# Hybrid state-space and attention block on one core: the down projection's last 256 tokens with tokens on partitions, their norm from a square root, and a new order of the first loads

## The chip, the cores and the metric

The kernel runs on 1 core of a Trainium2 chip. The metric is the device time of one execution in microseconds (us). Five engines work side by side, each through its own instructions in order: TensorE (PE, matrix products), VectorE (DVE), ScalarE (ACT), GpSimd (POOL) and SyncE (SP), which here does nothing but start DMA transfers between the chip's main memory and the on-chip memory. ACT and POOL can start transfers too. Engines wait for one another by semaphores. On-chip data lie on 128 partitions.

## The reference

One layer: a norm, a projection into two groups of heads (a diagonal state-space model and chunked attention with a window of 9 chunks of 64 frames), an output projection with a residual, a norm, a SwiGLU feed-forward layer with a residual, and a final norm over the 1024 features of each of 2048 tokens. Only the start and the end of it matter here:

```python
D_MODEL = 1024; SEQ = 2048; EPS = 1e-6

def rmsnorm(x, g):
    y = x * lax.rsqrt(jnp.mean(x * x, axis=-1, keepdims=True) + EPS)
    return y * g

# start:  h = rmsnorm(x, norm_mix_g) @ w_in
# end:    x = x + (silu(h2 @ w_gate) * (h2 @ w_up)) @ w_down
#         out = rmsnorm(x, norm_final_g)
```

All data are float32. Output: (1, 2048, 1024).

## The kernel before, in words

Activations lie with features on partitions and tokens along the free dimension: a tile is 128 features by up to 512 tokens. Each float32 operand of a large product is split into a rounded high part and a low part, and a product of two is three matrix instructions (high by high, high by low, low by high), which `mm3` issues at line 76. The transposes and the instructions at line 79 come from the same helper. Engines run in the order in which a scheduler has put the program; `tc.high_priority()` moves a group ahead there.

**Start.** `block_kernel` issues, all on SP: the three gains `g_mix`, `g_ffn`, `g_final` (L1666) and the relative bias `nbt` (L1670), which DVE negates (L1671) and SP stores back as `nbs` (L1672). `u_phase` then loads, for the first block of tokens, eight pairs of a weight tile `w` (L437) and an input tile `xt` (L441). ACT casts the weight's high part `wuh` (L438) and scales the input by `g_mix` into `raw` (L443); PE starts with the first pair.

**Middle.** The down phase and the gate and up phase before it fetch their operands with SP (`lo<-hc`, L1363, is 20 loads at the boundary after the output projection; `xt<-in_xt`, L1133, follows; DVE adds into `xt` at L1141, and PE's first `X<-hi,c` of the next phase waits for that).

**End.** `down_phase` walks the hidden features in groups and adds each group's product into the accumulators `acc` (8 tiles of 128 features by 1024 tokens, for each of two halves of the tokens). For the second half the last group of hidden features is kept back in the on-chip tiles `hs` and `ds`, and `TAIL` gives the order of what is left: three chunks of tokens, (first token, count) = (0, 512), (512, 256), (768, 256). I call them chunk 1, 2 and 3. For each chunk `down` makes tiles 0 to 3, then 4 and 5, then 6 and 7 of its 8 feature tiles, 12 matrix instructions a tile; DVE adds each into `acc` (L1575), ACT squares it (L1589, L1592), DVE adds the squares into `sa` and `sb` (L1593). Behind tiles 0 to 3 of a chunk come the `sums` of the chunk before it: PE sums the squares over the partitions by products with a column of ones, which puts tokens on partitions; `newton` turns that into the reciprocal root by 14 small DVE operations (L102 to L110, a bit trick and three Newton steps); behind tiles 4 and 5 PE spreads the root over all partitions by a transpose (L79), ACT copies it to `rs` (L141), and `products` multiplies each `acc` tile by gain and root on DVE (L1605) and stores it from SP (L1606). After chunk 3 there is no later chunk: its sums, root, products and stores follow one another.

Of the kernel before, what the change touches and what calls it, by code (L numbers as in the profile page):

```python
# [25 lines left out]
H, HD = 8, 64  # L26
# [4 lines left out]
HALF = 1024  # L31
# [20 lines left out]
ORDER = "sptf"  # L52
PINA = True
X1B = 6
TAIL = (0, 512), (512, 256), (768, 256)
MAGIC = 12582912.0
F2 = NF // 2
SB_, CB_, GB_ = 5, 5, 10
# [39 lines left out]
def newton(k, pool, ps, n, w):  # L98

    V = k.nc.vector  # L100
    v, f, y, o = (k.t(pool, t, [P, w], bufs=2) for t in ("nv", "nf", "ny", "no"))
    V.tensor_scalar(v[:], ps, 1.0 / n, EPS, op0=ALU.mult, op1=ALU.add)  # L102
    V.tensor_copy(f[:], v[:].bitcast(I32))
    V.tensor_scalar(f[:], f[:], -0.5, 1597463007.0, op0=ALU.mult, op1=ALU.add)
    V.tensor_copy(y[:].bitcast(I32), f[:])
    V.tensor_scalar(v[:], v[:], -0.5, None, op0=ALU.mult)
    for a, b in ((y, o), (o, y), (y, o)):
        V.tensor_tensor(f[:], a[:], a[:], op=ALU.mult)
        V.tensor_tensor(f[:], f[:], v[:], op=ALU.mult)
        V.scalar_tensor_tensor(b[:], f[:], 1.5, a[:], op0=ALU.add, op1=ALU.mult)  # L110
    return o


def tok_sums(k, te, ps, c, sq):

    for i in range(4):
        te.matmul(ps[:, c + i : c + i + 1], sq[:, i * P : (i + 1) * P], k.ones[:], start=True, stop=True)
# [5 lines left out]
        te.transpose(pb[:, i * P : (i + 1) * P], o[:, c + i : c + i + 1].to_broadcast([P, P]), k.ident[:])  # L123


def rstd_steps(k, te, psum, pool, tag, sq, n, out, nt=None, **kw):

    nt = nt or out.shape[-1] // P
    ps = k.t(psum, *tag, **kw)
    sqs = sq if isinstance(sq, list) else [sq]  # L130
    for i in range(nt):
        for m, sq in enumerate(sqs):
            te.matmul(ps[:, i : i + 1], sq[:, i * P : (i + 1) * P], k.ones[:], start=m == 0, stop=m == len(sqs) - 1)
    with k.tc.high_priority():
        o = newton(k, pool, ps[:, :nt], n, nt)
    yield
    pb = k.t(psum, *tag, **kw)
    for i in range(nt):
        te.transpose(pb[:, i * P : (i + 1) * P], o[:, i : i + 1].to_broadcast([P, P]), k.ident[:])
    if out is not None:  # L140
        k.nc.scalar.copy(out, pb[:, : nt * P])  # L141
    yield pb
# [255 lines left out]
def u_phase(k, ident, S, aw):  # L398
# [3 lines left out]
    with ExitStack() as cx:  # L402
# [98 lines left out]

        pro = ssm_prologue(k, ident, S)
        next(pro)
        held = [k.t(psum, "ps", [P, SB]) for _ in range(4)]

        def first(q):
# [3 lines left out]
        xs = [k.t(aw, "w", [P, 2, 1024], bufs=WB) for _ in range(2)]  # L510
        xns = cycle([x[:, m] for x in xs for m in range(2)])
        prep(BLOCKS[0], first)
        with tc.high_priority(offset=-LATER):
            next(pro)
        sums(BLOCKS[0])
# [991 lines left out]
def down_phase(k, S):  # L1507
    tc, nc, io = k.tc, k.nc, k.io
    V, te = nc.vector, k.te
    with ExitStack() as cx:  # L1510
# [67 lines left out]
        class End:  # L1578
# [13 lines left out]
                    nc.scalar.activation(t[:, :n], self.acc[i][:, self.ts], AF.Square)  # L1592
                    nc.vector.tensor_tensor(self.sa[m][:, :n], self.sa[m][:, :n], t[:, :n], op=ALU.add)  # L1593

            def sums(self, last=False):
                self.rs = None if last else k.t(fa, "rs", [P, 512])
                self.r = rstd_steps(k, k.te, dy, fa, ("ps", [P, 512]), self.sa, D, self.rs[:, : self.n] if self.rs else None, nt=self.n // P)
                next(self.r)

            def products(self):  # L1600
                pb = next(self.r)
                rs = self.rs or pb
                for i, a in enumerate(self.acc):
                    v = a[:, self.ts]
                    nc.vector.scalar_tensor_tensor(v, v, k.go[:, i : i + 1], rs[:, : self.n], op0=ALU.mult, op1=ALU.mult)  # L1605
                    nc.sync.dma_start(io["out"][i * P : (i + 1) * P, self.out], a[:, self.ts])  # L1606

        ends = []
        for hf in range(2):
            acc = []  # L1610
            f0 = 0
            for n, g in enumerate(DGROUPS[hf]):
                group(hf, f0, g, acc, (hf, n) == (0, 0))
                f0 += g
                if n in (0, 1):
                    for e in ends:
                        (e.sums, e.products)[n]()
            if hf == 0:
                ends = [End(hf, acc, t, 512) for t in (0, 512)]
                for e in ends:  # L1620
                    for i in range(KT):
                        e.square(i)
        hs, ds = zip(*((operand(S["h"][m : m + 1]), operand(S["wt"][m : m + 1])) for m in range(4)))
        last = None
        for t0, tn in TAIL:
            e = End(1, acc, t0, tn)
            for n, i in enumerate((0, 4, 6)):
                down(hs, ds, range(i, (4, 6, 8)[n]), acc, t0, tn, e)
                if last and n < 2:
                    (last.sums, last.products)[n]()  # L1630
            last = e
        last.sums(True)
        last.products()


def block_kernel(tc, io, phases="pusamf"):
    nc = tc.nc
    k = K(tc, io)
    k.ssm_eng = nc.gpsimd
    with ExitStack() as cx:  # L1640
        dram = cx.enter_context(tc.tile_pool(name="dram", bufs=1, space=bass.MemoryType.DRAM))
        cp = cx.enter_context(tc.tile_pool(name="const", bufs=1))
        k.t(cx.enter_context(tc.tile_pool(name="edge", bufs=1, side="right")), "edge", [P, 56])

# [12 lines left out]
        k.psum = None  # L1657
        k.names = {n: a.tensor.name for n, a in S.items()}
        ident = k.t(cp, "ident", [P, P])
        make_identity(nc, ident)  # L1660
        k.ident = ident
        k.ones = k.t(cp, "ones", [P, 1])
        nc.vector.memset(k.ones[:], 1.0)
        k.gm, k.gf, k.go = (k.t(cp, n, [P, KT]) for n in ("g_mix", "g_ffn", "g_final"))
        for n, g in (("g_mix", k.gm), ("g_ffn", k.gf), ("g_final", k.go)):
            nc.sync.dma_start(g[:], io[n])  # L1666
        S["rsn"] = k.t(cp, "rsn", [P, SEQ])
        with tc.tile_pool(name="nbp", bufs=1) as p:
            nbt = k.t(p, "nbt", [H, 768])
            nc.sync.dma_start(nbt[:], io["rel_bias"])  # L1670
            nc.vector.tensor_scalar(nbt[:], nbt[:], -1.0, None, op0=ALU.mult)  # L1671
            nc.sync.dma_start(S["nb"][:], nbt[:])  # L1672
        with tc.tile_pool(name="powers", bufs=1) as p:
            S["a8"] = k.t(p, "a8", [P, 2, NPR, 16])
            S["sw"] = k.t(p, "sw", [P, 3, 2, NPR])
            S["nba"] = k.t(p, "nba", [P, 640])
            with tc.tile_pool(name="apf", bufs=2, space=bass.MemoryType.PSUM, reuse_waits="tile") as k.pfs:
                pro, att = u_phase(k, ident, S, tc.alloc_tile_pool(name="aw", reuse_waits="tile", bufs=1, side="right"))
                mix = att.send(pro)
                for _ in att:  # L1680
                    pass
        with tc.tile_pool(name="mf", reuse_waits="tile", bufs=1) as mf:
            with pp() as psum, tc.tile_pool(name="mx", reuse_waits="tile", bufs=1) as mx:
                k.psum, k.mf, k.mx = psum, mf, mx
                for _ in mix:
                    pass
            gate_up_phase(k, S)
            down_phase(k, S)
    return k


def layout(inputs):
# [7 lines left out]
    def cols(v):  # L1700
        return np.ascontiguousarray(v.reshape(-1, P).T)
# [6 lines left out]
    def cg(v):  # L1708
# [6 lines left out]
        "x": x, "xt": a["x"][0].T, "xp": x.T, "w_u": cg(a["w_in"][0][:, :DS].T).T,  # L1715
        "w_qk": blocks(a["w_in"][0][:, DS : 3 * DS], D, P), "w_v": blocks(a["w_in"][0][:, 3 * DS :], D // 2, 256), "w_glu": cg(cg(a["ssm_w_glu"][0]).T).T, "w_out": np.concatenate([cg(a["w_out"][0][:DS]), a["w_out"][0][DS:]]),
        "w_gate": blocks(a["w_gate"][0], D, P), "w_up": blocks(a["w_up"][0], D, P), "w_down": a["w_down"][0],
        "g_mix": cols(a["norm_mix_g"][0]), "g_ffn": cols(a["norm_ffn_g"][0]), "g_final": cols(a["norm_final_g"]),
        "g_ssm": cols(cg(a["norm_ssm_out_g"][0])), "g_att": cols(a["norm_att_out_g"][0]), "b_glu": cols(cg(a["ssm_b_glu"][0])),
        "lam_re": pairs(a["ssm_lam_re"][0])[:, :, 0], "lam_im": pairs(a["ssm_lam_im"][0])[:, :, 0],  # L1720
        "log_dt": pairs(np.repeat(a["ssm_log_dt"][0][:, None], NS, 1))[:, :, 0],
# [24 lines left out]
```

## Time and profile before

| what | value |
|---|---|
| time, median of 3 runs | 2256.09 us (2250.8 to 2256.18) |
| the profiled execution's own time | 2247.43 us |
| its span in the trace | 2245.7 us |
| granted TensorE clock, mean | 0.988 |
| PE busy, share of the span | 96% |
| DVE, ACT, POOL busy | 69%, 45%, 16% |
| DMA, mean over the span | 192 GB/s |

A row of a timeline gives start, duration, engine, line, operation, output tile, input tiles, shapes, how many instructions were joined in the row, and in brackets how long the engine had been idle and what released it. "SPq" is SP starting a transfer. A duration covers an instruction from start to end; instructions of one engine overlap, so the distance between starts (or a joined row's length over its count) is the price of one more.

### The profile page before, as it was taken

To read this page: it belongs to the slowest core of one execution; us is meant where nothing else is said; L and a number is where in the kernel's file an instruction comes from. 1 tells how busy PE (TensorE), PEld (TensorE's weight loads), DVE (VectorE), ACT (ScalarE), POOL (GpSimd) and SP (SyncE) were. 2 spreads that over 40 slices of the span, in tenths; PEclk is the share of its full clock that TensorE was granted. 3 is DMA by queue.
4 is the path that set the end of the run, shared out by engine and by line. 5 is a ranking of instruction groups with operands and counts; after the bars stand their busy time and mean duration, and the time that the engine had idled before them with its cause. 6 is when DMAs were issued, how large, how long until landed. Compare 5 with 4: busy or idle time off the path is not lost.

```text
span 2245.7 us, 30154 instructions
## 1 busy us (share of the span) xinstructions
PE 2155.6 (96%) x10632; PEld 1817.4 (81%) x10632; DVE 1543.3 (69%) x2706; ACT 1004.6 (45%) x1667; POOL 352.4 (16%) x827
## 2 busy tenths in 40 slices
PE   8998899999997999999999999999999999999997
PEld 6777788899986788788888887888888788888886
DVE  7756666555557766777766678767666477689776
ACT  5455555556557642443333335333333343353322
POOL 2246576656500000000000000000000100000000
PEclk9999999999998999999999999999999999999999
DMA  8878876666652435845655557646333395465652
GB/s 281 251 244 275 280 220 204 202 192 199 190 166 99 155 113 181 288 136 155 198 168 194 191 182 268 210 144 213 117 100 112 122 383 192 160 228 177 220 175 76
DMA packets 194744, 430.16 MB, mean 192 GB/s; under 512 B 19872, under 2 KB 38352, under 8 KB 187488
## 3 DMA queue, kind: packets, MB, share of 16 engines
q1 hardware_dynamic: 186944, 403.32, 54.4%
q0 software_dynamic: 7648, 24.92, 3.6%
q8 instruction: 83, 1.36, 0.2%
q14 instruction: 69, 0.57, 0.1%
HBM read 288.95 MB, written 131.10 MB: 187 GB/s over the span
## 4 chain that ended last, share of the span: by engine, by line
PE 81%; DVE 7%; DMA 4%; ACT 3%; issue 2%; SPq 0%; DVEq 0%; ACTq 0%
PE X L76 20%; PE ps L76 19%; PE Y L76 10%; PE pf L76 10%; PE big L76 7%; PE W L76 5%; PE pj L76 4%; PE pt L79 2%; PE sc L76 2%; DMA lo<-hc 1%; DMA xt<-in_xt 1%; DVE ptl L893 1%; DMA x<-xt 0%; DVE s L874 0%; DVE lo L153 0%
## 5 line engine op out<-in xcount | busy, mean ns | idle before, releaser
L76 PE MATMUL X<-hi,c 128*128 128x512 f32 x1408 | 449.8, 390 | 6.7 <-DVE c L153 3.9
L76 PE MATMUL ps<-hd,hd 128*128 128x512 f32 (+1 forms) x1968 | 428.1, 379 | 3.1 <-DVE hd L153 2.0
L76 PEld LDWEIGHTS ps<-hd,hd 128*128 128x128 f32 x1968 | 356.4, 188 | 73.3 <-DVE hd L153 2.7
L76 PEld LDWEIGHTS X<-hi,c 128*128 128x128 f32 x1408 | 264.5, 188 | 63.2 <-DVE c L153 4.7
L76 PE MATMUL X<-lo,c 128*128 128x512 f32 x704 | 274.4, 390 | 0.0
L153 ACT CAST hd<-hd 128x1536 fp32r<-128x1536 f32 (+1 forms) x106 | 147.5, 1394 | 229.9 <-DMA hd<-hq 175.5
L76 PE MATMUL Y<-hi,c 128*128 128x512 f32 x704 | 224.8, 390 | 3.1 <-DVE u L1421 2.5
L153 DVE TENSOR_TENSOR hd<-hd 128x1536 fp32r<-128x1536 f32 (+1 forms) x106 | 174.0, 1643 | 38.0 <-ACT hd L153 37.7
L153 DVE TENSOR_TENSOR c<-S,c 128x512 fp32r<-128x512 f32 x176 | 120.8, 687 | 100.1 <-ACT c L153 99.8
L1525 POOL DMA_DIRECT2D hd<-hq x7 | 5.3, 755 | 1161.5 <-PE X L76 1148.8
L1417 ACT COPY u<-X 128x512 f32<-128x512 f32 x132 | 77.3, 586 | 197.7 <-PE X L76 197.7
L153 ACT CAST c<-S 128x512 fp32r<-128x512 f32 x176 | 109.4, 621 | 120.5 <-PE Y L76 61.6
L76 PE MATMUL big<-m,woh 128*128 128x512 f32 x512 | 160.1, 394 | 0.0
L76 PEld LDWEIGHTS Y<-hi,c 128*128 128x128 f32 x704 | 132.4, 188 | 31.9 <-DVE u L1421 3.3
L1559 DVE TENSOR_TENSOR acc<-acc,ps 128x512 f32<-128x512 f32 x196 | 129.6, 680 | 37.3 <-PE ps L76 37.1
L76 PEld LDWEIGHTS X<-lo,c 128*128 128x128 f32 x704 | 132.4, 188 | 27.4
L76 PE MATMUL pf<-hi,w 128*128 128x512 f32 x416 | 149.3, 411 | 0.0
L153 ACT CAST c<-raw 128x512 fp32r<-128x512 f32 x132 | 82.2, 623 | 147.7 <-PE Y L76 70.6
L76 PE MATMUL Y<-lo,c 128*128 128x512 f32 x352 | 137.2, 390 | 0.0
L893 DVE TENSOR_TENSOR ptl<-pt,pth 128x640 fp32r<-128x640 f32 (+3 forms) x152 | 98.2, 646 | 55.2 <-ACT pth L892 53.8
L877 ACT ACTIVATE s<-s,mn 128x640 f32<-128x640 f32 (+4 forms) x128 | 98.0, 765 | 61.1 <-DVE mn L874 57.7
L892 ACT CAST pth<-pt 128x640 fp32r<-128x640 f32 (+3 forms) x152 | 83.6, 550 | 84.2 <-PE pt L79 79.5
(448 smaller groups left out, 4267.9 us busy)
## 6 DMA issues: line engine op xcount, KB each, us to landing
w<-wss SPq DMA_DIRECT2D x36, 1024.0 KB, 6.1
hq<-g SPq DMA_DIRECT2D x140, 256.0 KB, 2.1
hd<-hq SPq DMA_DIRECT2D x35, 768.0 KB, 4.4
hd<-wc SPq DMA_DIRECT2D x35, 768.0 KB, 5.9
raw<-in_w_gate SPq DMA_DIRECT2D x44, 512.0 KB, 3.7
raw<-in_w_up SPq DMA_DIRECT2D x44, 512.0 KB, 4.1
wc<-px SPq DMA_DIRECT2D x66, 256.0 KB, 3.4
wss<-w SPq DMA_DIRECT2D x12, 1024.0 KB, 6.0
```

The lines of the kernel that those rows point to most:

```text
L76: return self.tc.keep_in_program_order(self.tc.nc.tensor.matmul(*a, **b))
L79: return self.tc.keep_in_program_order(self.tc.nc.tensor.transpose(*a, **b))
L153: return nc.scalar.copy(hi, raw), nc.vector.tensor_tensor(lo, raw, f32(hi), op=ALU.subtract)
L877: nc.scalar.activation(s[:, :nk], s[:, :nk], AF.Exp, bias=mn[:], scale=-1.0, accum_out=sums[sb, pr][:, hh, qp : qp + 1])
L892: nc.scalar.copy(pth[:, a:b, qp, :], pt[:, a:b, :])
L893: nc.vector.tensor_tensor(ptl[:, a:b, qp, :], pt[:, a:b, :], f32(pth[:, a:b, qp, :]), op=ALU.subtract)
L1417: nc.scalar.copy(u[:], ps[:])
L1525: (nc.gpsimd if aside else nc.sync).dma_start(f32(lo), src.rearrange("g p c -> p g c"))
L1559: V.tensor_tensor(a, a, ps[:], op=ALU.add)
```

## The change

Four edits.

1. **Chunk 3 becomes two blocks of 128 tokens** (`by_tokens`). The hidden activations are now the stationary operand and `w_down` the moving one, so that tokens lie on partitions and 512 features along the free dimension: 12 instructions of 128x512 for each half of the features. The residual in `acc` is added inside the accumulation, by 4 products of float32 `acc` tiles with the identity. ACT squares the result and sums it along the free dimension in one instruction; the root stays a column; DVE and ACT scale one half each and two transfers store a block, one from ACT and one from SP, into an output of its own, `out_t` (256 x 1024). The host puts the two outputs together. The gain is needed as a row on all partitions: one more SP load spreads `in_g_row` (4 KB) over 128 partitions of `rsn`. Chunk 2's `sums` and `products` move into the first block.
2. **The root** of chunks 1 and 2, and of the blocks, comes from ACT's Sqrt, DVE's reciprocal and one Newton step (`root`, `refine`). A Sqrt of a constant stands before the tail, so the function table is loaded there.
3. **The first loads**: SP starts with `w` and `xt`. `g_mix` is loaded from ACT, `nbt` and `nbs` go through POOL later, `g_ffn` and `g_final` follow block 1's loads on SP.
4. `eps` is a constant tile, set by DVE at the start.

```diff
-TAIL = (0, 512), (512, 256), (768, 256)
+TAIL = (0, 512), (512, 256)
+TOKENS = 768, 896
...
+def root(k, pool, ps, n, w):
+    v, f, y, o = (k.t(pool, t, [P, w], bufs=2) for t in ("nv", "nf", "ny", "no"))
+    k.nc.scalar.activation(o[:], ps, AF.Sqrt, scale=1.0 / n, bias=k.eps[:])
+    V.tensor_scalar(v[:], ps, -0.5 / n, -0.5 * EPS, op0=ALU.mult, op1=ALU.add)
+    return refine(V, v, f, y, o)
+
+def refine(V, v, f, y, o):
+    V.reciprocal(y[:], o[:])
+    V.tensor_tensor(f[:], y[:], y[:], op=ALU.mult)
+    V.tensor_tensor(f[:], f[:], v[:], op=ALU.mult)
+    V.scalar_tensor_tensor(o[:], f[:], 1.5, y[:], op0=ALU.add, op1=ALU.mult)
+    return o
...
+        nbt = k.t(p1, "nbt", [H, 768])
+        nc.gpsimd.dma_start(nbt[:], io["rel_bias"])
+        nc.vector.tensor_scalar(nbt[:], nbt[:], -1.0, None, op0=ALU.mult)
+        nc.gpsimd.dma_start(S["nb"][:], nbt[:])
...
         prep(BLOCKS[0], first)
+        for g, n in ((k.gf, "g_ffn"), (k.go, "g_final")):
+            nc.sync.dma_start(g[:], io[n])
...
+        def by_tokens(t0, hs, ds, acc):
+            ts = slice(t0, t0 + P)
...
+            g, ta = S["rsn"][:, :D], S["rsn"][:, D + m * 512 : D + m * 512 + 512]
...
+            for c in range(2):
+                for n, ((hh, hl), (dh, dl)) in enumerate(zip(hs, ds)):
+                    mm3(te, ps[c][:], hh[:, 0, ts], hl[:, 0, ts], dh[:, 0, c * 512 : c * 512 + 512], dl[:, 0, c * 512 : c * 512 + 512], n == 0, n == len(hs) - 1, skip_group_check=True)
+                    if n == 0:
+                        for i in range(4):
+                            te.matmul(ps[c][:, i * P : (i + 1) * P], acc[4 * c + i][:, ts], k.ident[:], start=False, stop=False, skip_group_check=True)
+                    if n % 2:
+                        yield
+                j = k.t(fa, "sg", [P, 512], bufs=2)
+                with tc.high_priority():
+                    nc.scalar.activation(j[:], ps[c][:], AF.Square, accum_out=sq[c][:])
+                    if c == 0:
+                        V.tensor_tensor(ta, ps[0][:], g[:, :512], op=ALU.mult)
+                        V.tensor_scalar(f[:], sq[0][:], 1.0 / D, EPS, op0=ALU.mult, op1=ALU.add)
+                        V.tensor_scalar(y[:], f[:], -0.5, None, op0=ALU.mult)
+            b = k.t(fa, "ob", [P, 512])
+            with tc.high_priority():
+                nc.scalar.activation(o[:], sq[1][:], AF.Sqrt, scale=1.0 / D, bias=f[:])
+                V.tensor_scalar(v[:], sq[1][:], -0.5 / D, y[:], op0=ALU.mult, op1=ALU.add)
+                refine(V, v, f, y, o)
+                nc.scalar.activation(ta, ta, AF.Copy, scale=o[:])
+                V.scalar_tensor_tensor(b[:], ps[1][:], o[:], g[:, 512:], op0=ALU.mult, op1=ALU.mult)
+            rows = slice(t0 - TOKENS[0], t0 - TOKENS[0] + P)
+            nc.scalar.dma_start(io["out_t"][rows, :512], ta)
+            nc.sync.dma_start(io["out_t"][rows, 512:], b[:])
+            yield
...
+        nc.sync.dma_start(S["rsn"][:, :D], bass.AP(io["g_row"].tensor, io["g_row"].offset, [[0, P], [1, D]]))
         hs, ds = zip(*(...))
+        nc.scalar.activation(k.t(fa, "q0", [P, 1], bufs=2)[:], k.eps[:], AF.Sqrt)
         for t0, tn in TAIL:
...
-                if last and n < 2:
-                    (last.sums, last.products)[n]()
+                if last and n == 0:
+                    last.sums(root=root)
+                if last and n == 1:
+                    last.products()
             last = e
-        last.sums(True)
-        last.products()
+        for t0 in TOKENS:
+            for n, _ in enumerate(by_tokens(t0, hs, ds, acc)):
+                if last and n == 1:
+                    last.sums(root=root)
+                if last and n == 2:
+                    last.products()
+                    last = None
...
+        k.eps = k.t(cp, "eps", [P, 1])
+        nc.vector.memset(k.eps[:], EPS)
...
-        for n, g in (("g_mix", k.gm), ("g_ffn", k.gf), ("g_final", k.go)):
-            nc.sync.dma_start(g[:], io[n])
+        nc.scalar.dma_start(k.gm[:], io["g_mix"])
...
-            nc.sync.dma_start(nbt[:], io["rel_bias"])
-            nc.vector.tensor_scalar(nbt[:], nbt[:], -1.0, None, op0=ALU.mult)
-            nc.sync.dma_start(S["nb"][:], nbt[:])
```

The order of the instructions is fixed when the program is built. Three places of it. First, SP at the program's start, before; the numbers in the names only tell tiles of one name apart:

```order
L1666 DMA g_mix_87<-in_g_mix 128x8
L1666 DMA g_ffn_88<-in_g_ffn 128x8
L1666 DMA g_final_89<-in_g_final 128x8
L1670 DMA nbt_97<-in_rel_bias 8x768
L437 DMA w_151<-in_w_u 128x512
L441 DMA xt_167<-in_xp 128x512
L437 DMA w_151<-in_w_u 128x512
L1672 DMA nbs_69<-nbt_97 8x768
L441 DMA xt_186<-in_xp 128x512
```

The same place now; the lines of the new kernel are numbered some 20 higher:

```order
L457 DMA w_147<-in_w_u 128x512
L461 DMA xt_163<-in_xp 128x512
L457 DMA w_147<-in_w_u 128x512
L461 DMA xt_182<-in_xp 128x512
L457 DMA w_147<-in_w_u 128x512
```

The first pair of tiles has moved from the fifth and sixth place to the first and second, and the second pair no longer has the store of `nbs` inside it.

Second, SP ahead of the 20 loads of `lo`, in the middle of the program, now (before, the last `hc` row is followed at once by the first `lo` row):

```order
L1168 DMA x_6_69<-xt_9849 128x2x512
L1342 DMA hc_74<-gh_2040_9948 128x512
L1342 DMA hc_74<-gl_2039_9946 128x512
L1684 DMA rsn_93<-in_g_row 128x1024
L1389 DMA lo_2046_10046<-hc_74 128x512
L1389 DMA lo_2052_10088<-hc_74 128x512
```

The scheduler has put the load of the gain's row here, more than 1200 us before the tail that reads it, and ahead of the `lo` loads.

Third, PE at the program's end. Before, from the last two feature tiles of chunk 3 (the rows of the last 24 products are cut to their last two) to the end; "x3" is one product of split operands:

```order
L76 MATMUL ps_19994<-hd_19527,hd_19531 128x256 x3
L76 MATMUL ps_19995<-hd_19527,hd_19531 128x256 x3
L76 MATMUL ps_20028<-ones_85,sa_19903 128x1
L76 MATMUL ps_20028<-ones_85,sb_19906 128x1
L76 MATMUL ps_20028<-ones_85,sa_19903 128x1
L76 MATMUL ps_20028<-ones_85,sb_19906 128x1
L79 MATMUL ps_20051<-ident_80,no_20036 128x128 x2
```

Now, the second half of the first block, into which chunk 2's sums and transposes have moved (the sums stand right ahead of it):

```order
L78 MATMUL ps_19868<-ones_87,sb_19727 128x1
L78 MATMUL ps_19844<-hd_19506,hd_19502 128x512 x3
L78 MATMUL ps_19844<-ident_82,acc_3278_18349 128x128
L78 MATMUL ps_19844<-ident_82,acc_3279_18350 128x128
L78 MATMUL ps_19844<-ident_82,acc_3280_18351 128x128
L78 MATMUL ps_19844<-ident_82,acc_3281_18352 128x128
L78 MATMUL ps_19844<-hd_19514,hd_19510 128x512 x3
L81 MATMUL ps_19898<-ident_82,no_19876 128x128 x2
L78 MATMUL ps_19844<-hd_19522,hd_19518 128x512 x3
L78 MATMUL ps_19844<-hd_19530,hd_19526 128x512 x3
```

PE's last instruction is now a large product of the second block, and no product with `ones` and no transpose follows it.

More of the change, by code (lines that the diff above doesn't have):

```diff
@@ L54 @@
 X1B = 6
-TAIL = (0, 512), (512, 256), (768, 256)
+TAIL = (0, 512), (512, 256)
+TOKENS = 768, 896
+TOK = SEQ - HALF + TOKENS[0]
 MAGIC = 12582912.0
@@ L111, in newton @@
     return o
+def root(k, pool, ps, n, w):
+    V = k.nc.vector
+    v, f, y, o = (k.t(pool, t, [P, w], bufs=2) for t in ("nv", "nf", "ny", "no"))
[8 more added lines that the diff above has]
+    return o
 def tok_sums(k, te, ps, c, sq):
@@ L123, in spread, with rstd_steps @@
         te.transpose(pb[:, i * P : (i + 1) * P], o[:, c + i : c + i + 1].to_broadcast([P, P]), k.ident[:])
-def rstd_steps(k, te, psum, pool, tag, sq, n, out, nt=None, **kw):
+def rstd_steps(k, te, psum, pool, tag, sq, n, out, nt=None, root=newton, **kw):
     nt = nt or out.shape[-1] // P
@@ L134, in rstd_steps @@
     with k.tc.high_priority():
-        o = newton(k, pool, ps[:, :nt], n, nt)
+        o = root(k, pool, ps[:, :nt], n, nt)
     yield
@@ L1593, in square, with sums @@
                     nc.vector.tensor_tensor(self.sa[m][:, :n], self.sa[m][:, :n], t[:, :n], op=ALU.add)
-            def sums(self, last=False):
-                self.rs = None if last else k.t(fa, "rs", [P, 512])
-                self.r = rstd_steps(k, k.te, dy, fa, ("ps", [P, 512]), self.sa, D, self.rs[:, : self.n] if self.rs else None, nt=self.n // P)
+            def sums(self, **kw):
+                self.rs = k.t(fa, "rs", [P, 512])
+                self.r = rstd_steps(k, k.te, dy, fa, ("ps", [P, 512]), self.sa, D, self.rs[:, : self.n], nt=self.n // P, **kw)
                 next(self.r)
             def products(self):
-                pb = next(self.r)
-                rs = self.rs or pb
+                next(self.r)
+                rs = self.rs
                 for i, a in enumerate(self.acc):
@@ L1606, in products @@
                     nc.sync.dma_start(io["out"][i * P : (i + 1) * P, self.out], a[:, self.ts])
+        def by_tokens(t0, hs, ds, acc):
+            ts = slice(t0, t0 + P)
+            m = (t0 // P) % 2
+            ps = [bank(dx) for _ in range(2)]
+            g, ta = S["rsn"][:, :D], S["rsn"][:, D + m * 512 : D + m * 512 + 512]
+            sq = [k.t(fa, f"q{c}", [P, 1], bufs=2) for c in range(2)]
+            v, f, y, o = (k.t(fa, n, [P, 1], bufs=2) for n in ("nv", "nf", "ny", "no"))
+            for c in range(2):
[24 more added lines that the diff above has]
+            yield
         ends = []
@@ L1664, in block_kernel @@
         k.gm, k.gf, k.go = (k.t(cp, n, [P, KT]) for n in ("g_mix", "g_ffn", "g_final"))
-        for n, g in (("g_mix", k.gm), ("g_ffn", k.gf), ("g_final", k.go)):
-            nc.sync.dma_start(g[:], io[n])
+        nc.scalar.dma_start(k.gm[:], io["g_mix"])
         S["rsn"] = k.t(cp, "rsn", [P, SEQ])
-        with tc.tile_pool(name="nbp", bufs=1) as p:
-            nbt = k.t(p, "nbt", [H, 768])
-            nc.sync.dma_start(nbt[:], io["rel_bias"])
-            nc.vector.tensor_scalar(nbt[:], nbt[:], -1.0, None, op0=ALU.mult)
-            nc.sync.dma_start(S["nb"][:], nbt[:])
         with tc.tile_pool(name="powers", bufs=1) as p:
@@ L1717, in layout @@
         "w_gate": blocks(a["w_gate"][0], D, P), "w_up": blocks(a["w_up"][0], D, P), "w_down": a["w_down"][0],
-        "g_mix": cols(a["norm_mix_g"][0]), "g_ffn": cols(a["norm_ffn_g"][0]), "g_final": cols(a["norm_final_g"]),
+        "g_mix": cols(a["norm_mix_g"][0]), "g_ffn": cols(a["norm_ffn_g"][0]), "g_final": cols(a["norm_final_g"]), "g_row": a["norm_final_g"].reshape(1, D),
         "g_ssm": cols(cg(a["norm_ssm_out_g"][0])), "g_att": cols(a["norm_att_out_g"][0]), "b_glu": cols(cg(a["ssm_b_glu"][0])),
@@ L1740 @@
         io[name] = nc.dram_tensor(f"in_{name}", a.shape, mybir.dt.from_np(a.dtype), kind="ExternalInput").ap()
-    io["out"] = nc.dram_tensor("out", (D, SEQ), F32, kind="ExternalOutput").ap()
+    io["out"] = nc.dram_tensor("out", (D, TOK), F32, kind="ExternalOutput").ap()
+    io["out_t"] = nc.dram_tensor("out_t", (SEQ - TOK, D), F32, kind="ExternalOutput").ap()
     with tile.TileContext(nc) as tc:
@@ L1744 @@
     r = run_bass_kernel_spmd(nc, [arrays], core_ids=[0])
-    return np.ascontiguousarray(r.results[0]["out"].T)[None]
+    return np.ascontiguousarray(np.concatenate([r.results[0]["out"].T, r.results[0]["out_t"]]))[None]
```

## The prediction

> **What bounds the kernel now.** I read the page first, then the chain of what ended last, then timelines at the three places that the change touches. Busy time and chain:
>
> ```profile
> PE 2155.6 (96%) x10632; PEld 1817.4 (81%) x10632; DVE 1543.3 (69%) x2706; ACT 1004.6 (45%) x1667; POOL 352.4 (16%) x827
> PE 81%; DVE 7%; DMA 4%; ACT 3%; issue 2%; SPq 0%; DVEq 0%; ACTq 0%
> ```
>
> PE is busy 96% of the span. A change can pay only by removing PE work or by shortening the 90 us in which PE stands still. The tail, on PE's timeline:
>
> ```profile
> 2208.68 0.95 PE L76 MATMUL ps<-ones,sa 128*128 128x1 f32 x8
> 2209.49 3.11 PE L76 MATMUL ps<-hd,hd 128*128 128x256 f32 x24
> 2213.82 0.65 PE L79 MATMUL ps<-ident,no 128*128 128x128 f32 x4 [1.21 <-DVE no L110]
> 2214.22 8.88 PE L76 MATMUL ps<-hd,hd 128*128 128x256 f32 x72
> ...
> 2228.26 0.43 PE L79 MATMUL ps<-ident,no 128*128 128x128 f32 x2 [1.40 <-DVE no L110]
> 2228.45 3.10 PE L76 MATMUL ps<-hd,hd 128*128 128x256 f32 x24
> 2234.08 0.38 PE L76 MATMUL ps<-ones,sa 128*128 128x1 f32 x2 [2.52 <-DVE sa L1593]
> ...
> 2237.85 0.66 PE L79 MATMUL ps<-ident,no 128*128 128x128 f32 x2 [2.72 <-DVE no L110]
> ```
>
> PE's last large product ends at 2228.45 + 3.10 = 2231.55. The span ends at 2245.7, so 14.15 us follow with no large product in them. Before that, PE waits twice for a root (1.21 and 1.40). What fills the 14.15 us stands in the chain, and on DVE and SP:
>
> ```profile
> 2232.82 0.42 ACT sg L1592
> 2235.17 0.17 DVE nv L102
> ...
> 2237.54 0.17 DVE no L110
> 2238.55 3.22 DVE L1605 SCALAR_TENSOR_TENSOR acc<-acc,g_final,ps 128x256 f32<-128x256 f32 x8 [0.84 <-PE ps L79]
> 2215.90 27.32 SPq L1606 DMA_DIRECT2D out<-acc  x24
> ```
>
> Squares and their sums until 2235.17; Newton's 14 small steps until 2237.7; transposes; eight products until 2241.77; SP starts the last store until 2215.90 + 27.32 = 2243.22; it has landed at 2245.7, 2.5 us behind that.
>
> **The tail.** First the durations for what is new:
>
> ```profile
> 288.80 1.89 PE L76 MATMUL pj<-rsn,Bst 128*128 128x256 f32 x8
> 290.34 0.50 PE L76 MATMUL sc<-k,q2h 128*128 128x320 f32 x1
> 1781.49 0.62 PE L76 MATMUL W<-hi,c 128*128 128x512 f32 x2
> ...
> 1782.17 0.62 PE L76 MATMUL W<-hi,c 128*128 128x512 f32 x2
> 2203.23 1.31 ACT L1592 ACTIVATE sg<-acc 128x512 f32<-128x512 f32 x2 [4.13 <-DVE acc L1575]
> 2215.12 5.39 DVE L1605 SCALAR_TENSOR_TENSOR acc<-acc,g_final,rs 128x512 f32<-128x512 f32 x8 [1.03 <-ACT rs L141]
> L877 ACT ACTIVATION_READ_ACCUMULATOR s<-s,mn 128x1 f32 x128 | 24.1, 188 | 0.0
> ```
>
> A split product of 512 columns costs (1782.17 - 1781.49) / 3 = 0.227 us an instruction, one of 256 columns 3.11 / 24 = 0.13, or 8.88 / 72 = 0.123 in a long run. A product with unsplit float32 operands shows as two instructions (the order's 4 rows of `ones` are the trace's 8). At 256 columns such an instruction costs (290.34 - 288.80) / 8 = 0.19, at one column 0.95 / 8 = 0.12. The identity products have 128 columns: I take 0.12, since the price barely falls with the columns; the ends are half of the 256-column row, 0.10, and that row itself, 0.19. The two blocks have 16 such products, 32 instructions: 3.8 us (3.1 to 6.1).
>
> Step by step on the old time axis:
> - Chunk 1's root. Its sums end at 2209.63. Sqrt on ACT runs beside `nv` on DVE; then four DVE steps, which Newton's chain spaces at some 0.2 (2235.17 to 2237.54 for 13 starts), and they queue behind DVE's additions as before. Ready near 2211.5, while the 24 products last until 2212.6. The stall of 1.21 goes; what is late next is nothing, PE runs on.
> - Chunk 2's tiles 6 and 7, 24 x 0.123, end at 2216.0.
> - First half of block 1: 12 x 0.227 + 8 x 0.12 = 3.7, to 2219.7.
> - Chunk 2's sums. They need DVE's `sa`, and DVE first works off chunk 1's products, 5.39 us. With the stall gone these start at 2213.9 and end at 2219.3; then two additions (0.7), ACT's square (0.42), two more additions (0.8): 2221.2. PE stalls 1.5 here, a new wait in place of the two old ones; in before, four feature tiles of chunk 3 covered it. Sums 1.0: 2222.2.
> - Second half 3.7 and two transposes 0.4: 2226.3. Chunk 2's products (3.3 on DVE) and the first block's own root and scaling lie under the second block, 2 x 3.7: PE ends at 2233.7, 2.1 later than before.
> - Behind it: Square 0.65 and the read of its sum 0.19, to 2234.6; Sqrt of one column 0.2; four DVE steps 0.8; the last half's product 0.67 (5.39 / 8) beside ACT's Copy: 2236.4 with the waits between. The store's start 0.4 and 2.5 of landing for 128 KB, and for two stores of 256 KB together, 384 KB more, at most 1.0 at the 413 GB/s worked out below; I take half: 2239.8.
>
> So the end falls from 2245.7 to 2239.8, and I enter **-5.9 us**. Ends: identity products 0.7 less or 2.3 more, the stall 1.5 less, the store 0.5 either way: -8.6 to -3.1.
>
> [...]
>
> **The table and the Sqrt's first use.**
>
> ```profile
> L1058 ACT ACT_TABLE_LOAD x6 | 7.7, 1283 | 0.1
> 1779.01 0.61 ACT L153 CAST c<-raw 128x512 fp32r<-128x512 f32 x1
> 1781.30 0.59 ACT L1417 COPY u<-X 128x512 f32<-128x512 f32 x1 [1.67 <-PE X L76]
> 1786.73 0.58 ACT L1417 COPY u<-X 128x512 f32<-128x512 f32 x1 [4.85 <-PE X L76]
> ```
>
> One load more, 1.28, and a one-column activation, 0.2, stand between the first two rows of the timeline, where ACT idles 1.67 us. I enter 0. Without that cover the copy would be late by 1.5 us, and 4.85 us of idle follow it.
>
> **The gain's row.** It goes into SP's queue ahead of the 20 `lo` loads:
>
> ```profile
> 914.54 12.70 SPq L1363 DMA_DIRECT2D lo<-hc  x20
> 926.92 5.15 DMA lo<-hc
> 943.03 0.47 PE L76 MATMUL X<-hi,c 128*128 128x512 f32 x1 [1.79 <-DVE xt L1141]
> 905.00:930.00 25.00, 24.73 (x116) 20.35 (x115) 18.41 (x39) 11.09 (x19) 0.00 (x0) 1.00 0.99 315
> nba<-nbs SPq DMA_DIRECT2D x32, 144.0 KB, 4.5
> ```
>
> (The row of a window has the busy time of PE, PEld, DVE, ACT and POOL, then the granted clock, the DMA engines' busy share and GB/s.) The 20 loads of 256 KB (128x512 floats) leave at 12.70 / 20 = 0.635 us each, which is 413 GB/s, with the DMA engines busy 0.99: there is no room. Their last piece lies on the chain (926.92 to 932.07), then `hi`, and behind more steps the `xt` for which PE has waited 1.79 us at 943.03. So what the row's 512 KB take, PE waits longer: 512 KB at 413 GB/s, **+1.3 us**; at the 315 GB/s of the stretch 1.7, and 0 if it slips into a gap of the queue.
>
> **The first loads.**
>
> ```profile
> 0.74 0.38 SPq L1666 DMA_DIRECT2D g_mix<-in_g_mix  x1
> ...
> 2.53 0.36 SPq L437 DMA_DIRECT2D w<-in_w_u  x1
> 2.93 0.43 SPq L441 DMA_DIRECT2D xt<-in_xp  x1
> ...
> 4.46 0.30 SPq L1672 DMA_DIRECT2D nbs<-nbt  x1
> 4.80 0.34 SPq L441 DMA_DIRECT2D xt<-in_xp  x1
> 6.72 0.72 ACT L443 ACTIVATE raw<-xt,g_mix 128x512 fp32r<-128x512 f32 x1 [0.80 <-DMA xt<-in_xp]
> 7.49 1.58 PE L76 MATMUL ps<-raw,wuh 128*128 128x512 f32 x2 [7.49 <-ACT raw L443]
> ...
> 34.03 1.13 SPq L549 DMA_DIRECT2D nba<-nbs  x1
> 40.00:70.00 30.00, 27.61 (x122) 21.69 (x121) 20.30 (x68) 16.70 (x30) 7.58 (x12) 1.00 0.92 276
> ```
>
> `raw` waits for `xt`, PE for `raw`. `w` now starts at 0.74 and not at 2.53, `xt` with it: 1.8 us earlier. The second `xt` starts near 2.0 and not at 4.80, since the store of `nbs`, which waits for DVE, is gone from between; that is no gain of its own, as PE has four times three products to do with the first pair. `g_mix` comes from ACT's queue at 0.74, beside the table load, and lands before `xt`. I round to **-2.0 us** for PE's start. It carries through only if the later loads come earlier as well: in 40 to 70 us the DMA engines are busy 0.92 and PE 27.61 of 30, so what sets PE's waits there is the stream of loads, and this too starts 1.8 us earlier. Against it: `g_ffn` and `g_final` (0.4 us of SP each) now stand ahead of the second block's loads, and DVE's order in the first 100 us is shuffled. The bias goes through POOL, whose `nbs` store waits for DVE's negation, now among the splits of the first pairs; its reader on SP starts at 34.03, so it has tens of us; were it later than that, SP's queue of loads would stand behind it, us for us. I enter 0 for it. Ends: -0.5 and -2.8, the whole gain of the second pair.
>
> **The sum.** -2.0 + 1.3 + 0 - 5.9 = **-6.6 us** on the span of 2245.7, to 2239.1; the profiled execution of 2247.43 would be 2240.8. The median of 2256.09 lies 8.7 above that execution, and I take the change over to it: **2249.5 us**, -0.29%. I call no change what lies within 0.3%, 6.8 us, about what a measurement of this kernel can tell: the three runs before are 5.4 us apart. The forecast sits on that edge, so its chance divides between faster and same.
>
> **Rivals.**
>
> *The row's load holds the queue* (slower than before). 128 packets read the same 4 KB, and nothing in the trace of before reads like that in this size. The nearest row is `nba<-nbs`, 144 KB that read overlapping rows, 4.5 us to landing: 33 GB/s if all of that were rate, and 512 KB would take 16.0 us. The `lo` loads behind it, and PE at 943.03, would be late by that. The sum would be -6.6 - 1.3 + 16.0 = +8.1: 2264.2. It decides from 7.9 us of transfer on (then the kernel is no faster), and passes 0.3% at 14.7. Against it: 128 KB stores land in 2.5 us, so most of the 4.5 is likely not rate; and the packets are 4 KB long. Chance 0.08.
>
> *The start does not carry through and PE's tail is dear*. The loads of block 2, behind two more small ones, come no earlier, so PE meets the old wait: head -0.5. Identity products at 0.19: 2.3 more. Sum -0.5 + 1.3 - 3.6 = -2.8: 2253.3. For it: DMA shares of 0.9, where a queue that starts earlier also fills earlier. Chance 0.22.
>
> *Everything overlaps better*. The row slips into a gap, the head brings 2.8, and DVE is quick enough with chunk 1's products that the sums' stall of 1.5 is gone: -2.8 + 0 - 7.4 = -10.2: 2245.9. For it: the second pair's 2.8 us, if the first blocks wait for loads throughout. Against it: DVE has all eight products ahead of `sa` in its order, and the DMA share of 0.99 leaves no gap for the row. Chance 0.16.
>
> *A change without effect*: if PE's start were not at 5.5 but at 7.5, because `g_mix` on ACT lands late, and the last stores were no shorter than 8 us behind the root, the sum would be near 0. 0.04.
>
> **How the numbers follow.** Forecast 0.48, half of it beyond the edge of 6.8 us: faster 0.24 + 0.16 and 0.05 of the dear tail's better end, 0.45. Slower 0.08 and the 0.02 left for what I do not see: 0.10. The rest is same, 0.45. Range: the upper case 2245.9 less 3.4 for the spread of medians (half of 5.4, and the tail's cheapest products, 0.7): 2242.5. Upwards the dear case 2253.3 and half that spread, 2.7, and 2.5 for a row's load that takes 4: 2258.5. The slow row lies outside.
>
> **What the profile would show.** Right: PE's first product near 5.5; the wait at the start of `X<-hi,c` some 3.1 instead of 1.79; no wait ahead of chunk 1's transposes; one wait of some 1.5 ahead of chunk 2's `ones`; identity products 0.12 apart; 6 us from PE's last product to the end, not 14. Wrong: a first product after 7; `lo` loads spaced out behind the row by over 4 us; identity products over 0.19; a Sqrt that waits for a second table load in the tail; more than 8 us behind PE's last product.

## The result, and the profile after

The changed kernel takes 2271.91 us (median of 6 runs, 2268.01 to 2273.76), the kernel before 2252.7 (6 runs, 2247.04 to 2256.18): ratio 1.0082 [1.0068, 1.0097] (in brackets the 95% interval), some 19 us slower. The forecast was 2249.5, with 2258.5 as the upper end. The profiled execution has a span of 2270.3 us, 24.6 more than before's; before's was a quick one, 5.3 us under that kernel's median, so the two traces lie further apart than the medians.

PE's share is the same, its busy time is not. The page of the changed kernel, PE and the chain:

```profile
PE 2188.6 (96%) x10606; PEld 1824.9 (80%) x10606; DVE 1535.2 (68%) x2671; ACT 1007.3 (44%) x1675; POOL 353.4 (16%) x829
PE 74%; DVE 4%; DMA 2%; ACT 1%; issue 1%; SPq 0%; DVEq 0%; ACTq 0%
```

33.0 us more busy time (2155.6 before) with 26 instructions fewer: PE does not wait longer (it stands still 81.7 us now, 90.1 before), it works more slowly. Where, the windows tell. A long stretch of the gate and up phase, before:

```profile
1450.00:1700.00 250.00, 250.00 (x1105) 207.01 (x1104) 166.59 (x255) 91.46 (x158) 0.00 (x0) 1.00 0.45 147
```

and after:

```profile
1450.00:1700.00 250.00, 250.00 (x1073) 201.24 (x1073) 161.64 (x247) 89.11 (x154) 0.00 (x0) 1.00 0.45 149
```

PE is busy throughout in both, at a granted clock of 1.00, with the DMA engines equally busy (0.45). It gets through 1105 products before and 1073 now: 0.2262 us and 0.2330 us each. The phase has 3696 such products (`X`, `Y` and `W` from `hi`, `lo` and `c`), so by the price this costs 3696 x 0.0068 = 25 us. No edit touches a line of this phase. From its first product to its last, before and after:

```profile
943.03:1793.70 850.67, 842.68 (x3709) 695.73 (x3709) 583.74 (x914) 333.59 (x571) 3.54 (x5) 1.00 0.51 168
949.73:1821.90 872.17, 866.46 (x3709) 696.45 (x3709) 585.91 (x914) 335.03 (x573) 3.64 (x5) 1.00 0.50 165
```

PE is busy 23.8 us longer, and the phase lasts 21.5 us longer, because PE stands still in it 5.7 us and not 8.0. That is about the whole of what the kernel has lost.

At the places that the edits do touch, things went mostly as forecast. PE's start and the wait behind the gain's row:

```profile
5.91 1.60 PE L78 MATMUL ps<-raw,wuh 128*128 128x512 f32 x2 [5.91 <-ACT raw L463]
...
949.73 0.47 PE L78 MATMUL X<-hi,c 128*128 128x512 f32 x1 [2.89 <-DVE xt L1167]
```

7.49 became 5.91, and the wait of 1.79 became 2.89. SP at the row, and ACT at the table load:

```profile
919.92 0.43 SPq L1684 DMA_DIRECT2D rsn<-in_g_row  x1
920.44 13.61 SPq L1389 DMA_DIRECT2D lo<-hc  x20
```

```profile
1806.82 0.61 ACT L173 CAST c<-raw 128x512 fp32r<-128x512 f32 x1
1807.44 1.28 ACT L1686 ACT_TABLE_LOAD   x1
1808.74 0.20 ACT L1686 ACTIVATE q<-eps 128x1 f32<-128x1 f32 x1
1809.18 0.59 ACT L1443 COPY u<-X 128x512 f32<-128x512 f32 x1 [0.23 <-PE X L78]
```

The table load fits into the idle stretch: `u` still waits 0.23 us for PE. The tail on PE, from chunk 1's sums:

```profile
2236.97 0.95 PE L78 MATMUL ps<-ones,sa 128*128 128x1 f32 x8
2237.78 3.10 PE L78 MATMUL ps<-hd,hd 128*128 128x256 f32 x24
2240.72 0.60 PE L81 MATMUL ps<-ident,no 128*128 128x128 f32 x4
...
2249.43 0.38 PE L78 MATMUL ps<-ones,sa 128*128 128x1 f32 x2 [1.56 <-DVE sa L1619]
...
2251.12 1.49 PE L78 MATMUL ps<-ident,acc 128*128 128x128 f32 x8
2252.26 1.63 PE L78 MATMUL ps<-hd,hd 128*128 128x512 f32 x3
2253.69 0.63 PE L81 MATMUL ps<-ident,no 128*128 128x128 f32 x2
...
2260.26 1.05 PE L78 MATMUL ps<-ident,acc 128*128 128x128 f32 x8
2261.07 2.30 PE L78 MATMUL ps<-hd,hd 128*128 128x512 f32 x9
```

No wait ahead of chunk 1's transposes, one of 1.56 ahead of chunk 2's `ones`. From the start of chunk 1's sums to the end of the span it is 2270.3 - 2236.97 = 33.3 us, against 2245.7 - 2208.68 = 37.0 before. In the middle of it three large products take 2253.69 - 2252.26 = 1.43 us and not 0.68 (3 x 0.227). The windows from the wait on say why:

```profile
2247.87:2249.43 1.56, 0.00 (x0) 0.00 (x1) 1.29 (x4) 1.05 (x3) 0.00 (x0) 1.00 0.93 357
2249.43:2250.34 0.91, 0.91 (x8) 0.91 (x9) 0.49 (x1) 0.39 (x2) 0.00 (x0) 1.00 0.00 0
2250.34:2254.80 4.46, 4.46 (x20) 3.84 (x20) 1.03 (x9) 0.64 (x2) 0.00 (x0) 0.64 0.00 0
...
2252.30:2253.70 1.40, 1.40 (x6) 1.00 (x6) 0.00 (x0) 0.00 (x0) 0.00 (x0) 0.50 0.00 0
2253.70:2255.00 1.30, 1.30 (x6) 1.11 (x5) 0.24 (x1) 0.37 (x1) 0.00 (x0) 0.50 0.00 0
```

Behind the wait and the small sums the granted clock is 0.64 over 4.5 us, and 0.50 where the three products lie.

### The profile page after: what moved, and what is told of

Its sections match the earlier page's. It is cut to its first block, busy times and chain, and to the rows that moved or that the text cites. A ratio compares the mean times of both kernels' runs of the same rounds, so it can differ in the third digit from the quotient of the medians.

```text
span 2270.3 us, 30073 instructions
## 1 busy us (share of the span) xinstructions
PE 2188.6 (96%) x10606; PEld 1824.9 (80%) x10606; DVE 1535.2 (68%) x2671; ACT 1007.3 (44%) x1675; POOL 353.4 (16%) x829
## 4 chain that ended last, share of the span: by engine, by line
PE 74%; DVE 4%; DMA 2%; ACT 1%; issue 1%; SPq 0%; DVEq 0%; ACTq 0%
PE X L78 21%; PE ps L78 19%; PE Y L78 11%; PE big L78 6%; PE pf L78 6%; PE W L78 5%; PE pj L78 3%; PE pt L81 2%; PE sc L78 1%; DMA x<-xt 1%; DVE lo L173 1%; DVE xt L1167 0%; DMA yr<-y 0%; DVE m L173 0%; DMA hc<-gh 0%
## 5 line engine op out<-in xcount | busy, mean ns | idle before, releaser
L78 PE MATMUL X<-hi,c 128*128 128x512 f32 x1408 | 459.2, 397 | 7.2 <-DVE c L173 3.8
L78 PE MATMUL X<-lo,c 128*128 128x512 f32 x704 | 279.0, 396 | 0.0
```

Of the source, the lines that this page charges most:

```text
L78: return self.tc.keep_in_program_order(self.tc.nc.tensor.matmul(*a, **b))
```

## The experiments

What had changed in the slow phase, if not its instructions? In the built programs the first of the five tiles `c`, the stationary operand there, starts 56,320 bytes into a partition before and 56,352 now; the moving operands `hi` and `lo`, allocated from the right end of the memory, stand where they stood. The 32 bytes are the constant `eps`: a float32 column, padded, allocated ahead of everything on the left.

**Is it the address, and which?** Four runs move tiles and leave the instructions alone, but for one small DVE write to the pad in the second.

`eps` of 64 bytes:

```diff
-        k.eps = k.t(cp, "eps", [P, 1])
+        k.eps = k.t(cp, "eps", [P, 16])[:, :1]
```

> The changed kernel, with the constant eps in a tile of 16 columns (64 bytes a partition) where it has 1 (32 bytes with padding); every tile allocated behind it moves 32 bytes up again, so the tiles c of the gate and up phase start on a multiple of 64 bytes as in the kernel before. Address theory (the products of the gate and up phase, 3696 with c as the stationary operand, are 0.0067 us dearer each because c stands 32 bytes off): the distance of two products falls from 0.233 to 0.227, some 25 us go, time 2247, about 6 under the kernel before. Rival (the edits themselves slow PE in that phase, through the gain's row, the shifted start or another order of the loads): 0.233 and 2272 stay.

Measured: 2271.64, ratio to the kernel before 1.0091 [1.0073, 1.0109]. Still slow. Taken alone this speaks for the rival.

The kernel before, with the phase's own pool moved:

```diff
         gb = cx.enter_context(tc.tile_pool(name="gb", reuse_waits="tile", bufs=1))
+        pad = k.t(gb, "pad", [P, 1])
+        V.memset(pad[:], EPS)
```

> The kernel before, with one unused column tile ahead in the pool of the gate and up phase that holds c, S, u and g; these tiles move up by 32 bytes and nothing else changes. Address theory: 0.233 between products there, 25 us more, about 2277. Rival (the edits): nothing, 2253.

Measured: 2274.7, 1.0104 [1.0086, 1.0122]. With none of the edits, 32 bytes make the kernel before as slow as the changed one. The rival is out; what fell with the run ahead of it is only that 64 would be as good as 0.

Both operands moved by 32, and the moving one by 32 with `c` by 64:

```diff
-        k.t(..., "edge", [P, 56])
+        k.t(..., "edge", [P, 48])
```

> The changed kernel with the pad tile at the right edge of the memory cut from 56 to 48 columns, so that the tiles hi and lo (the moving operand in the gate and up phase) and hd (both operands in the down phase) move up by 32 bytes; c stays 32 bytes off. If only the stationary operand's own address counts: the gate and up phase stays at 0.233, and the down phase goes there too (hd is its stationary operand), 13 us more, 2285. If the offset between the two operands counts: the gate and up phase returns to 0.227 and the down phase stays, 2247. Edits rival: 2272.

Measured: 2252.13, 1.0004 [0.9991, 1.0018]: fast again.

> The changed kernel with the eps tile of 64 bytes and the right edge's pad of 48 columns: c on a multiple of 64, hi, lo and hd 32 bytes off. If the stationary operand's own address counts: 0.227 in the gate and up phase, 0.233 in the down phase, about 2260. If the offset between the operands counts: 0.233 in the gate and up phase, 0.227 in the down phase, 2272. If the moving operand's address counts: both slow, 2285.

Measured: 2275.61, 1.0111 [1.009, 1.0132], which is the pattern of the offset between the operands (the absolute level was expected 3.6 lower). The down phase, whose two operands move together, stays as it was in both: 619 or 620 products between 1900 and 2040 us, as in the two kernels.

**Is it these operands, and what is the period?**

```diff
+        pads = []
...
+                if not pads:
+                    pads.append(k.t(gb, "pad", [P, 1]))
+                    V.memset(pads[0][:], EPS)
                 u = k.t(gb, "u", [P, 512], bufs=4)
```

> The kernel before, with the unused column tile allocated behind c: u and g of the gate and up phase move up by 32 bytes, c and S stay. If the products' operand c is what counts: distance 0.226 to 0.227 there, about 2252. If it is what ACT and DVE write and read beside PE (u, g): 0.233, 2277.

Measured: 2252.74, 0.9995 [0.9985, 1.0006]. Moving `u` and `g`, which ACT and DVE write and read beside PE, does nothing. The tiles `S`, which DVE writes and from some of which `c` is split, moved with `c` in every run and were not tried apart from it.

`eps` of 128 and of 256 bytes (`[P, 32]`, `[P, 64]`):

> The changed kernel with eps in a tile of 32 columns, 128 bytes: c stands 128 bytes on from where it was, hi and lo as before. Steps of 32 and 64 bytes were slow. If the pattern repeats every 128 bytes: 0.227, about 2248. If it repeats every 256 or more: 0.233, 2272.

> The changed kernel with eps in a tile of 64 columns, 256 bytes. If the pattern repeats every 128 or 256 bytes: 0.227, about 2248. If every 512 or more: 0.233, 2272.

Measured: 2270.76, 1.0073 [1.0053, 1.0092] at 128 bytes, and 2250.68, 0.999 [0.9977, 1.0003] at 256. The same window of 250 us in these seven kernels, in the order `eps` 64, before with `c` 32, both 32, `c` 64 with `hi` 32, before with `u` 32, `eps` 128, `eps` 256:

```profile
1450.00:1700.00 250.00, 250.00 (x1073) 200.33 (x1073) 161.31 (x246) 89.33 (x154) 0.00 (x0) 1.00 0.45 148
```
```profile
1450.00:1700.00 250.00, 250.00 (x1073) 201.44 (x1072) 163.45 (x250) 89.06 (x153) 0.00 (x0) 1.00 0.46 152
```
```profile
1450.00:1700.00 250.00, 250.00 (x1105) 207.01 (x1104) 167.84 (x257) 91.74 (x157) 0.00 (x0) 1.00 0.45 150
```
```profile
1450.00:1700.00 250.00, 250.00 (x1073) 201.25 (x1072) 162.38 (x248) 89.37 (x154) 0.00 (x0) 1.00 0.45 150
```
```profile
1450.00:1700.00 250.00, 250.00 (x1104) 207.13 (x1104) 167.56 (x257) 91.69 (x157) 0.00 (x0) 1.00 0.45 148
```
```profile
1450.00:1700.00 250.00, 250.00 (x1074) 201.19 (x1073) 163.47 (x250) 88.84 (x153) 0.00 (x0) 1.00 0.46 152
```
```profile
1450.00:1700.00 250.00, 250.00 (x1104) 207.08 (x1103) 166.72 (x255) 92.27 (x158) 0.00 (x0) 1.00 0.46 155
```

There are only two values, 1073 or 1074 products and 1104 or 1105. The offset of `c` against `hi`, relative to the kernel before, is 0 in the fast kernels, or 256 bytes; 32 (three kernels), 64 and 128 are slow. In bytes, one of the `hi` less the first `c` is 122,624 - 56,320 = 66,304, a multiple of 256. In the kernel before all `c`, `hi` and `lo` start on multiples of 256; with all of them 32 bytes off (both 32) it is as fast, so it is the difference that counts. Between 1000 and 1300 us, at a clock of 1.00, it is the same: 1327 products in seven fast kernels (the one before, both 32, before with `u` 32, `eps` 256 and three of those below), 1289 or 1290 in the five slow ones.

**What are the edits worth without it?** `eps` goes into the unused pad tile, and all tiles keep their old places:

```diff
-        k.eps = k.t(cp, "eps", [P, 1])
-        k.t(..., "edge", [P, 56])
+        k.eps = k.t(..., "edge", [P, 56])[:, :1]
```

> All four edits, with the constant eps in the first column of the pad tile that lay unused at the right edge, so that every other tile has the address it had in the kernel before. Address theory: distance of two products in the gate and up phase 0.227, about 20 us under the changed kernel; and what the edits themselves are worth is read here: -6.6 by the prediction's sum, 2246; near 2252 if the earlier run with both operands shifted (2252.1) tells their worth. Rival (the edits slow PE): 2272.

Measured: 2248.35, 0.9981 [0.9968, 0.9995]; 0.0019 x 2252 = 4.3 us under the kernel before. Two of the kernels above also have all four edits at a fast offset, and show less: +0.9 us with both operands moved (1.0004) and -2.3 with `eps` 256 (0.9990). So the edits are worth something between nothing and 4 us.

The loads' order alone, put into the kernel before:

> The kernel before with the new order of the first loads alone (the gains, the bias; tail, root and eps as before). Prediction: -2.0, about 2250. If the start is made good for by later waits: 0, 2252.

Measured: 2253.16, 1.0000 [0.9990, 1.0011]. PE starts 1.9 earlier, and at the first score product it is 0.5 ahead of the kernel before:

```profile
5.62 1.72 PE L76 MATMUL ps<-raw,wuh 128*128 128x512 f32 x2 [5.62 <-ACT raw L443]
...
134.76 0.45 PE L76 MATMUL sc<-hi2x,hi0x 128*128 128x128 f32 x1 [4.21 <-DVE hi2x L806]
```

The kernel before has that product at

```profile
135.30 0.45 PE L76 MATMUL sc<-hi2x,hi0x 128*128 128x128 f32 x1 [4.21 <-DVE hi2x L800]
```

But 0.5 is less than what separates one profile from the next: this product starts at 133.4 to 136.2 in seven profiles with the new order of the loads, and at 134.2 to 135.3 in three with the old one. By then no lead can be told.

The tail alone:

> The blocks, the root and the gain's row without the new order of the first loads, eps in the edge's pad tile. Prediction: -5.9 + 1.3 = -4.6, 2247. From the timeline of the run with both operands shifted (tail 3.8 shorter, the wait for xt 0.5 to 1.1 longer): -3, 2249.

Measured: 2247.04, 0.9981 [0.9971, 0.9990]. The tail alone gives as much as all the edits.

The gain's row later:

```diff
...
+        q0 = k.t(fa, "q0", [P, 1], bufs=2)
+        nc.scalar.activation(q0[:], k.eps[:], AF.Sqrt)
+        nc.vector.tensor_copy(S["rsn"][:, :1], q0[:])
         nc.sync.dma_start(S["rsn"][:, :D], bass.AP(...))
```

> All four edits at the old addresses, and the gain's row loaded only behind the first Sqrt at the start of the down phase (one DVE copy of one column makes it wait), away from the 20 loads of lo. If the row costs what the wait for xt shows: that wait back at 1.8, 1.1 us under all edits at the old addresses. If the row is free there: the same time.

Measured: 2247.88, 0.9985 [0.9976, 0.9994]. The wait for `xt` is back at 1.4, but the time is that of all edits at the old addresses, within what the intervals can tell. The head-only kernel, which has no such load, waits 2.5 there, so a good part of the 2.89 is not the row's: this wait is 1.4 to 2.5 in four profiles without the row there (mean 2.0) and 2.3 to 3.2 in six with it (mean 2.8). In this run's own profile the tail is 1.5 us longer than in that of all edits, because the low clock lasts longer (0.50 over 5.6 us, against 0.50 over 2.3 us in all edits, with 0.78 and 0.86 before and behind), so the time does not settle what the row is worth.

**The stall that the change brought.** Chunk 2's sums and products move on by one step of `by_tokens`:

```diff
-                if last and n == 1:
+                if last and n == 2:
                     last.sums(root=root)
-                if last and n == 2:
+                if last and n == 3:
                     last.products()
```

> All edits at the old addresses, and chunk 2's sums moved from the end of the first block's first half into its second half, its products behind that half. The trace of the changed kernel has PE waiting 1.56 for sa there, and then 3.9 us at a granted clock of 0.50 to 0.72, which cost some 1.7. If the low clock follows from the wait: both go, 3 us under all edits at the old addresses, 2245, and the clock stays 1.00 in the tail. If the low clock comes anyway, from the sums' small products: 1.5 us. If DVE is then late with the second block's work: nothing, 2248.

Measured: 2245.55, 0.9959 [0.9946, 0.9973]: by the ratio 9.2 us under the kernel before, by the medians 7.0, and faster than both kernels. Against all edits at the old addresses the intervals just overlap, so this step is read from the traces. PE in its tail, and two windows:

```profile
2213.29 0.95 PE L78 MATMUL ps<-ones,sa 128*128 128x1 f32 x8
...
2226.30 0.28 PE L78 MATMUL ps<-ones,sa 128*128 128x1 f32 x2
...
2227.11 1.65 PE L78 MATMUL ps<-hd,hd 128*128 128x512 f32 x6
2228.60 0.38 PE L81 MATMUL ps<-ident,no 128*128 128x128 f32 x2
```
```profile
2220.00:2226.00 6.00, 6.00 (x38) 5.31 (x37) 5.48 (x11) 1.29 (x4) 0.00 (x0) 1.00 0.90 347
2226.00:2232.00 6.00, 6.00 (x36) 5.13 (x36) 4.06 (x18) 1.79 (x8) 0.00 (x0) 1.00 0.13 44
```

No wait, PE busy throughout, the clock at 1.00, although the sums' small products are the same. The span ends at 2243.1, 29.8 us behind the start of chunk 1's sums (33.3 in the changed kernel). So the sums alone did not bring the low clock. Nor did a wait alone: in the kernel before, the waits of 1.21 and 1.40 have large products behind them but for a transpose, and the clock there is 1.00, though these waits are a little shorter. In the tail it came where a wait of 1.55 or 1.56 and the sums stood together, down to 0.50 in six profiles (the changed kernel, both 32, `eps` 256, all edits at the old addresses, the tail alone, the row later); in the `eps` 64 run, with a wait of 1.59 and the same sums, it did not. That one prices it: from the start of chunk 1's sums to the end of PE's last product it is 24.8 us there and 26.4 in the changed kernel, 1.6 for the low clock; without wait and low clock it is 23.0.

## Why the prediction was wrong

- **The step that failed** is the one that was not taken: the fourth edit, `eps` as a constant tile, has no term in the sum, and no rival speaks of it. I priced instructions, waits and transfers, and took for granted that a product costs the same wherever its operands lie. It cost 25 us by the price of a product, and made a phase that the diff does not touch 21.5 us longer. The runs show it from both sides: added to the kernel before (+1.04%), taken out of the changed kernel (from 1.0082 to 0.9981).
- **The tail**: entered at -5.9, on the two timelines -3.7. The root's wait went and the sums' wait came, 1.56 against 1.5. Two sizes were off. PE's last product ends 2261.07 + 2.30 - 2236.97 = 26.4 us behind the start of chunk 1's sums, and I had 25.0: the low clock behind the wait (24.8 without it, in the `eps` 64 run), against which the identity products were cheaper (8 in 0.81 at full clock, 0.10 each, not 0.12). And from PE's end to the span's end it is 6.9, not 6.1: SP has started the last store by 2259.51 + 6.89 = 2266.40, and the end comes 3.9 later, where I had 3.0. The store itself is not late. The rows of the transfers give KB and the median time to landing, now and, in the last row, before:

```profile
2259.51 6.89 SPq L1666 DMA_DIRECT2D out_t<-ob  x2
out_t<-rsn ACTq DMA_DIRECT2D x2, 256.0 KB, 2.5
out_t<-ob SPq DMA_DIRECT2D x2, 256.0 KB, 2.6
out<-acc SPq DMA_DIRECT2D x16, 128.0 KB, 2.0
```

So the 2.5 that I took for a landing before was some 2.0 of landing and a rest up to the end of the span, and this rest grew to 1.3 or more. What fills it is not shown.
- **The first loads**: the start came as forecast (-1.6 and -1.9), the -2.0 for the whole kernel did not: 1.0000 [0.9990, 1.0011] allows some 2.5 us either way, so the time alone does not rule it out, but by 135 us no lead can be told. The rival that the start does not carry through fits this; that the stream of loads gives it back, its reason, is not shown.
- **The gain's row**: +1.3 forecast; the wait grew by 1.1 between the two profiles and by some 0.8 between the means of those without and with the row there; moving the row's load brought nothing that the intervals show. The slow row (16 us) is out: `lo` left in 13.61 instead of 12.70.
- **The table load**: 0, as forecast.
- Summed, the edits without the address are worth -4.3 (interval -7.2 to -1.1), against a forecast of -6.6; the two other kernels with all edits at a fast offset say +0.9 (-2.0 to +4.1) and -2.3 (-5.2 to +0.7).
- Two smaller slips: the base of 2256.09 was 3.4 over the 2252.7 that six runs gave, and in the upper end a row's load of 4 us is 4 - 1.3 = 2.7 over the sum, not 2.5.

## What to carry to other kernels

A new tile, 32 bytes with its padding, moved every tile allocated behind it (`c` from 56,320 to 56,352): compare the addresses of the operands of the hot products before and after a change, and put new constants where nothing moves. When a change is slower and no wait has grown, count instructions per window at a clock of 1.00; a product's price that differs by 3% in an untouched phase is seen there in one line (1105 against 1073). And a short wait of PE can be dearer than it reads, here by 1.6 us more for a wait of 1.56 with the small sums behind it: look at the granted clock behind it.

## What of the hardware was not expected

- A float32r product of 128x128 by 128x512 took 0.2262 us or 0.2330 us by the offset between its stationary and its moving tile: fast where the offset was the old one or 256 bytes on, slow at 32, 64 and 128. Why is not shown, and the other multiples of 32 were not tried.
- A wait of PE of 1.56 us, followed by 0.9 us of one-column products, was followed by a granted clock of 0.50 for some 3 us; in the `eps` 64 run, with a wait of 1.59, the clock stayed at 1.00 there:

```profile
2254.20:2256.50 2.30, 2.30 (x16) 1.98 (x15) 0.40 (x4) 0.37 (x1) 0.00 (x0) 1.00 0.00 0
```
